# Decode attention values as float32 on four column tiles, with unsplit V and loads in pools of their own

## The chip, the cores and the metric

The kernel runs on one core of one Trainium2 chip. TensorE multiplies matrices, VectorE and ScalarE do elementwise work and reductions, GpSimd does small elementwise work and issues some DMAs, SyncE issues the other DMAs. The metric is the device time of one execution in microseconds, as the median of several runs. The program is recorded by a layer that orders the instructions of each engine at build time, with priorities and a planned timeline; on the chip each engine then runs its own list strictly in that order and waits on semaphores.

## What is computed

One step of a streaming encoder with two layers, for 1024 new frames of one prompt stream and for 16 new frames of each of 8 running streams (the decode part). The change concerns layer 0 of the decode part only: differential attention of 16 queries per stream against 1024 cached and 16 new keys and values, in 4 heads. Each head has two softmax maps, whose difference weighs the values:

```python
def _diff_attn(q, k, v, q_pos, k_pos, rel_bias, lam):
    s = jnp.einsum('bqhcd,bkhcd->bhcqk', q, k).astype(jnp.float32) * (A_HALF_DIM ** -0.5)
    bias = rel_bias[_t5_bucket(k_pos[None, :] - q_pos[:, None])]
    s = s + jnp.transpose(bias, (2, 0, 1)).astype(jnp.float32)[None, :, None]
    ...
    p = jax.nn.softmax(s, axis=-1)
    w = p[:, :, 0] - lam * p[:, :, 1]
    return jnp.einsum('bhqk,bkhe->bqhe', w.astype(v.dtype), v)
...
    o = _rmsnorm(o, subln_g) * (1.0 - LAMBDA_INIT_0)
    out_a = o.reshape(bsz, t, A_WIDTH) * jax.nn.silu(g_a)
    ...
    y = x + jnp.einsum('bte,ed->btd', jnp.concatenate([out_a, out_b], axis=-1), w_out)
```

All inputs are float32. The cached keys and values of one stream are 2 MiB each, and every one of them is read once from HBM.

## The kernel before

The program goes through the input projection, the attention and gating of the prompt (`phase_prompt`), the decode stage (`phase_decode`, prepared by `decode_begin`), and the convolution layer (`phase_conv`). Large products are done in the type float32r, with each operand split into a high and a low part and three products per pair (`mm3`, line 157). Small products are done in float32, and each of these shows as two instructions in the trace.

The decode stage does two things at once. The first is the attention of the eight streams, called sequences here. The second is the output projection of layer 0 for the tiles of 128 tokens: `prep` loads and transposes a tile, `main` multiplies it (48 products of 512 columns, tile "out"), adds the residual and normalises. One pass of the loop over b, a period, takes scores of sequence b, keys of b+1, values of b-1, the projection of tile b-2 and the weights of b. The steps of a sequence are:

- `keys_part`: four loads of 512 KiB from the key cache into tiles "raw", issued by SyncE. These tiles come from the pool `rawp` of three buffers, which the loads of the output weights (`split_w`, line 139) and of `prep` share. TensorE transposes them (line 417), and VectorE and ScalarE copy the result to KT.
- `dscores`: scores of the 4 heads, each head on its own 32 columns of TensorE, so on four column tiles (line 731), in three PSUM tiles S; then maxima (736), exponents (744) and sums.
- `dweights`: nine products of the exponents with `cf`, which holds the normaliser and the sign of each map, give the weights with the keys on the partitions (759), 64 columns for 4 heads of 16 queries. They are split into a high and a low part (762, 763).
- `dvalues`: four loads of V into "vraw", two buffers, issued by GpSimd (773). ScalarE makes the high part vh (776), VectorE the low part vl (777). The weights of all heads are multiplied with all 512 columns of V (784, 785, 787), so that three quarters of the result belong to a wrong head; a mask `own` takes them out (789), a product with `place` moves the sequence to its rows (791), and VectorE adds it to `oacc` (795).
- `dfinish`: once for all sequences, the norm per head, the gate from `s_ga`, and the store to `s_oa`, which `prep(8)` reads.

The product of weights and values in the code is this:

```python
                    if k < 8:
                        nc.tensor.matmul(pav, lhsT=wt[:, k, :], rhs=x, start=(k == 0), stop=False)
                    nc.tensor.matmul(pav[:64], lhsT=wt[:, k, :64], rhs=y, start=False, stop=False)
```

What sets the order around it is the recording order of the loop, moved by the planned timeline: the trace of before shows the value products of one sequence in several pieces between "out" products and key transposes, and the scores of a sequence in up to five pieces.

## Time and profile before

| | us |
|---|---|
| median of 3 runs (lowest, highest) | 1223.09 (1223.04, 1224.46) |
| profiled execution | 1223.68 |
| its span, first to last instruction | 1221.9 |
| TensorE busy in the span | 1156.0 |
| VectorE, ScalarE, GpSimd busy | 731.6, 456.8, 340.7 |
| mean granted clock of TensorE, as a share of 2.4 GHz | 0.979 |

The times of the runs are of whole executions; the profile is of one more execution, and its span leaves out 1.8 us before the first and after the last instruction. A matmul's record lasts longer than its share of TensorE, since matmuls are pipelined, so costs are read from the distance of starts. "Idle" in a row is the time in which an engine did nothing just before an instruction, with what released it.

### The profile page before, as it was taken

What the parts mean: (1) busy time and instruction counts of PE and PEld (TensorE: products, weight loads), DVE (VectorE), ACT (ScalarE), POOL (GpSimd) and SP (SyncE); (2) the same over time, 40 slices, a digit from 0 to 9 for tenths busy, and PEclk for the clock granted to TensorE, in tenths of its full rate; (3) what the DMA queues carried; (4) which work ended last, traced back from release to release, by engine and by line L of the source; (5) the groups of instructions that cost most, each with busy time, mean ns of one, the idle gap of its engine ahead of it and who ended that gap; (6) DMA issues with size and microseconds to landing.
All of it is one profiled execution on the core that took longest, in us unless ns stands there. A gap on an engine that the chain in (4) does not pass through costs nothing. (4 is left out here: it accounts for less than half of the span.)

```text
span 1221.9 us, 20908 instructions
## 1 busy us (share of the span) xinstructions
PE 1156.0 (95%) x7886; PEld 1024.1 (84%) x7886; DVE 731.6 (60%) x1560; ACT 456.8 (37%) x1065; POOL 340.7 (28%) x510
## 2 busy tenths in 40 slices
PE   6999999999989998679999999999999999998997
PEld 4878998899989997457777677899999899996886
DVE  4420225678788878766556444698999711377443
ACT  4431223445454545555444334312121222365221
POOL 2233223334434435413322231212131220350000
PEclk9999999999989998879999999999999999998999
DMA  8453435324132313867767635333332442113331
GB/s 302 110 169 91 144 118 172 107 71 121 46 89 78 108 50 105 301 214 242 258 226 255 192 125 190 92 91 96 93 96 90 140 134 84 35 35 104 104 104 69
DMA packets 125365, 160.33 MB, mean 131 GB/s; under 512 B 16514, under 2 KB 87194, under 8 KB 125257
## 3 DMA queue, kind: packets, MB, share of 16 engines
q1 hardware_dynamic: 109344, 106.95, 28.5%
q0 software_dynamic: 15776, 51.79, 12.9%
q8 instruction: 62, 1.02, 0.3%
q14 instruction: 39, 0.31, 0.1%
q10 hardware_dynamic: 144, 0.26, 0.1%
HBM read 119.41 MB, written 40.00 MB: 130 GB/s over the span
## 5 line engine op out<-in xcount | busy, mean ns | idle before, releaser
L157 PE MATMUL mm<-yh,wh 128*128 128x384 f32 x576 | 196.5, 341 | 3.3 <-ACT sb L1133 2.5
L157 PE MATMUL mm<-yl,wh 128*128 128x384 f32 x576 | 193.9, 337 | 0.5 <-issue 0.5
L157 PE MATMUL mm<-yh,wl 128*128 128x384 f32 x576 | 193.8, 338 | 0.3 <-DVE wl L146 0.2
L157 PE MATMUL mm<-wh,xh 128*128 128x384 f32 (+1 forms) x504 | 185.4, 369 | 2.5 <-DVE sg L468 1.4
L157 PE MATMUL mm<-wl,xh 128*128 128x384 f32 (+1 forms) x504 | 184.5, 366 | 0.9 <-DVE wl L146 0.9
L157 PE MATMUL mm<-wh,xl 128*128 128x384 f32 (+1 forms) x504 | 183.7, 364 | 0.0
L146 DVE TENSOR_TENSOR wl<-raw,wh 128x1024 fp32r<-128x1024 f32 (+1 forms) x72 | 84.3, 1178 | 104.7 <-ACT wh L145 102.7
L1173 DVE SCALAR_TENSOR_TENSOR cT<-u,cc,cT 128x128 f32<-128x128 f32 (+1 forms) x180 | 141.3, 843 | 1.0
L157 PEld LDWEIGHTS mm<-yh,wh 128*128 128x128 f32 x576 | 108.7, 189 | 6.2 <-issue 2.8
L157 PEld LDWEIGHTS mm<-yh,wl 128*128 128x128 f32 x576 | 108.6, 189 | 2.0 <-DVE wl L146 0.9
L157 PEld LDWEIGHTS mm<-yl,wh 128*128 128x128 f32 x576 | 108.7, 189 | 1.1 <-issue 0.7
L157 PEld LDWEIGHTS mm<-wh,xh 128*128 128x128 f32 x504 | 95.7, 190 | 13.3 <-DVE sg L468 1.4
L157 PEld LDWEIGHTS mm<-wl,xh 128*128 128x128 f32 x504 | 95.9, 190 | 10.5 <-DVE wl L146 1.8
L157 PEld LDWEIGHTS mm<-wh,xl 128*128 128x128 f32 x504 | 95.7, 190 | 8.7 <-DVE xl L170 0.3
L145 ACT CAST wh<-raw 128x1024 fp32r<-128x1024 f32 (+1 forms) x72 | 71.8, 1001 | 73.0 <-PE mm L157 30.9
L126 POOL TENSOR_TENSOR rr<-pw,mhalf 128x1 f32<-128x1 f32 x59 | 33.0, 559 | 200.3 <-DVE pw L125 190.8
L559 ACT ACTIVATE e<-S,nm 128x512 f32<-128x512 f32 (+5 forms) x96 | 55.1, 579 | 42.1 <-DVE nm L554 26.4
L157 PE MATMUL out<-wh,ch 128*128 128x512 f32 x144 | 59.9, 416 | 2.0 <-DVE xr L845 1.2
L157 PE MATMUL mm<-wh,ch 128*128 128x512 f32 x144 | 57.1, 397 | 4.5 <-ACT ch L1079 4.5
L551 DVE TENSOR_REDUCE nm<-S 128x1 f32<-128x512 f32 (+5 forms) x96 | 52.5, 551 | 12.6 <-PE S L546 11.9
L777 DVE TENSOR_TENSOR vl<-vraw,vh 128x1024 fp32r<-128x1024 f32 x32 | 43.2, 1351 | 26.8 <-ACT vh L776 26.6
L157 PE MATMUL out<-wh,cl 128*128 128x512 f32 x144 | 58.8, 408 | 0.0
(282 smaller groups left out, 2300.6 us busy)
## 6 DMA issues: line engine op xcount, KB each, us to landing
raw<-in_cache_k SPq DMA_DIRECT2D x32, 512.0 KB, 4.4
vraw<-in_cache_v POOLq DMA_DIRECT2D x32, 512.0 KB, 5.7
raw<-in_w_in SPq DMA_DIRECT2D x24, 512.0 KB, 5.3
raw<-in_w_out SPq DMA_DIRECT2D x16, 512.0 KB, 5.0
raw<-in_w_in SPq DMA_DIRECT2D x32, 256.0 KB, 4.0
raw<-in_w_in SPq DMA_DIRECT2D x48, 128.0 KB, 2.8
s_y<-xr POOLq DMA_DIRECT2D x9, 512.0 KB, 4.7
x<-s_y SPq DMA_DIRECT2D x9, 512.0 KB, 4.3
```

The source lines that it names most:

```text
L126: m = nc.gpsimd.tensor_tensor(out, v[:, :w], self.mhalf[:, :w], ALU.pow)
L145: nc.scalar.copy(h[:, :ks * n], raw[:, :ks * n])
L146: (low or nc.vector).tensor_tensor(l[:, :ks * n], raw[:, :ks * n], h[:, :ks * n].bitcast(F32), ALU.subtract)
L157: m = self.nc.tensor.matmul(out, lhsT=x, rhs=y, start=(i == 0), stop=(i == n - 1))
L551: nc.vector.tensor_reduce(nm[:, j:j + 1], s[:, :n], AX.X, ALU.max, negate=True)
L559: nc.scalar.activation(e[:, j * n:(j + 1) * n], S[j][:, :n], AF.Exp, bias=nv, accum_out=zz[:, j:j + 1])
L777: (nc.vector if i in VDVE else nc.gpsimd).tensor_tensor(vl, vr, vh.bitcast(F32), ALU.subtract)
L1173: nc.vector.scalar_tensor_tensor(dst, src, w1, dst, ALU.mult, ALU.add)
```

## The change

The value product no longer works with split operands. V is used as it is loaded, the weights are kept as one float32 tile, and each head's 16 weight columns are multiplied with its own 128 columns of V only, on the column tile of that head, so that no mask and no placing are needed: the result of a sequence stands with head h at partitions 32h to 32h+15. The norm and the gate are done for each sequence right behind its values, from a gate tile `gs` in the same layout, and `og` is stored to `s_oa` in two portions. The sum over keys runs backwards (the new keys' tile first, then tiles 7 to 0).

The four score products are called in one group with a higher priority, the values too. Key loads get a pool of five buffers of their own (`krp`), value loads one of six (`vp`), now allocated on the other side of the memory, and `vload(b)` is called behind `dvalues(b - 1)`, `vload(0)` ahead of the loop. The pool of PSUM tiles for the weights falls from two buffers to one; one PSUM tile `pvt` holds two value results and two ninth weight columns. The constants `own` and `place` are no longer loaded.

```diff
+HPS = 300
+VB = 6
+KB = 5
...
-        vp = E(tc.tile_pool(name="vp", bufs=2, side="right", reuse_waits="tile"))
+        krp = E(tc.tile_pool(name="krp", bufs=KB, side="right", reuse_waits="tile"))
...
+            nc.gpsimd.memset(gs, 0.0)
+            for h in range(H):
+                nc.sync.dma_start(out=gs[h * 32:h * 32 + NQ], in_=self.s_ga[T:, h * P:(h + 1) * P].rearrange(
+                    "(b q) e -> q b e", q=NQ))
+            nc.sync.dma_start(out=vs, in_=self.v0s)
...
-                kr = self.rawp.tile([P, 1024], F32, name="raw").rearrange("p (t c) -> p t c", t=2)
+                kr = krp.tile([P, 1024], F32, name="kraw").rearrange("p (t c) -> p t c", t=2)
...
+        vp = dec.enter_context(tc.tile_pool(name="vp", bufs=VB, reuse_waits="tile"))
+        pm = E(tc.tile_pool(name="pa", bufs=1, space=PSUM, reuse_waits="tile"))
+        pvp = E(tc.tile_pool(name="pvp", bufs=1, space=PSUM, reuse_waits="tile"))
+        pvt = pvp.tile([P, 512], F32, name="pv")
...
-            for i, parts in enumerate(((0, 1), (2,), (3,))):
-                s = pS.tile([P, 512], F32, name="S")
-                for j, p in enumerate(parts):
+            S = [pS.tile([P, 512], F32, name="S") for _ in range(3)]
+            with tc.high_priority(offset=HPS):
+                for p, i, j in ((3, 2, 0), (2, 1, 0), (0, 0, 0), (1, 0, 1)):
...
-            wt = ep.tile([P, 9, P], F32R, name="wt", bufs=1)
...
+            wt = ep.tile([P, 9, 64], F32, name="wt", bufs=2)
+            ps = pm.tile([P, 512], F32, name="mm")
+            p8 = pvt[:, 256 + b % 2 * 64:320 + b % 2 * 64]
+            for k in range(9):
+                nc.tensor.matmul(ps[:, k * 64:(k + 1) * 64] if k < 8 else p8, lhsT=ex[:, k, :], rhs=cf,
+                                 start=True, stop=True)
+            nc.scalar.copy(wt[:, :8], ps.rearrange("p (k e) -> p k e", e=64))
+            nc.vector.tensor_copy(wt[:, 8], p8)
...
+        def vload(b):
...
+            for i in range(4):
+                vr = vp.tile([P, 1024], F32, name="vraw").rearrange("p (t c) -> p t c", t=2)
+                nc.gpsimd.dma_start(out=vr, in_=cv[:, 2 * i:2 * i + 2])
+                seqs[b]["V"] += [vr[:, 0], vr[:, 1]]
...
+            pav = pvt[:, b % 2 * P:(b % 2 + 1) * P]
+            with tc.high_priority(offset=HPS):
+                for k in range(8, -1, -1):
+                    for h in range(H):
+                        nc.tensor.matmul(pav[h * 32:h * 32 + NQ], lhsT=wt[:, k, h * NQ:(h + 1) * NQ],
+                                         rhs=V[k][:, h * P:(h + 1) * P], start=(k == 8), stop=(k == 0))
             jk = ep.tile([P, P], F32, name="jk", bufs=1)
...
+            nc.scalar.activation(jk, pav, AF.Square, accum_out=ss)
...
             self.rpow(rm, ss, 1.0 / P, 1e-6)
...
+            nc.vector.scalar_tensor_tensor(og[:, b], pav, rm, gs[:, b], ALU.mult, ALU.mult)
+            if b >= NB - 2:
...
+                    nc.sync.dma_start(out=self.s_oa[T:, h * P:(h + 1) * P].rearrange("(b q) e -> q b e", q=NQ)[:, bs],
+                                      in_=og[h * 32:h * 32 + NQ, bs])
...
+        vload(0)
         for b in range(NB):
...
                 dvalues(b - 1)
+                vload(b)
...
-        dfinish()
```

Where the instructions come to stand is told by the built programs. TensorE at the opening of the decode stage, before: S is a score tile, `tr<-cst,raw` key transposes, and the rows on lines 784 and 785 are the values of sequence 0.

```order
L417 MATMUL tr<-cst_58,raw 128x128 x8
L731 MATMUL S<-KT,qz_5782 32x256 x4
L784 MATMUL mm<-vh,wt 128x512
L785 MATMUL mm<-vl,wt 64x512
L784 MATMUL mm<-vh,wt 128x512
L785 MATMUL mm<-vl,wt 64x512
L784 MATMUL mm<-vh,wt 128x512
L417 MATMUL tr<-cst_58,raw 128x128 x8
L731 MATMUL S<-KT,qz_5782 32x256 x4
L785 MATMUL mm<-vl,wt 64x512
```

The same place now: lines 739, 766 and 789 are scores, weights and values.

```order
L766 MATMUL mm<-cf,ex 128x64 x8
L766 MATMUL pv<-cf,ex 128x64
L739 MATMUL S<-KTx,qz_5782 32x272 x4
L789 MATMUL pv<-vs,wt 16x128 x4
L789 MATMUL pv<-vraw,wt 16x128 x32
L739 MATMUL S<-KT,qz_5782 32x256 x12
L766 MATMUL mm<-cf,ex 128x64 x8
L766 MATMUL pv<-cf,ex 128x64
L789 MATMUL pv<-vs,wt 16x128 x4
L789 MATMUL pv<-vraw,wt 16x128 x32
L766 MATMUL mm<-cf,ex 128x64 x2
L170 MATMUL tr<-cst_58,raw 128x128 x4
```

The values of a sequence now stand in one piece, the scores in one group but for the piece of the last keys here, and the values of sequences 0 and 1 both stand ahead of the first "out" product. GpSimd behind the exponents' zeroing of sequence 1, before, with the semaphores that each row waits for:

```order
L739 MEMSET ex_6178 128x128 [waits PE_49,Activation_49,Pool_49]
L773 DMA vraw_6432<-in_cache_v0 128x2x512 [waits DMASW7_49,DVE_49]
L773 DMA vraw_6442<-in_cache_v0 128x2x512 [waits DMASW0_49,DVE_49]
L704 COPY KTx_6559<-kts_5774 128x4x16
L773 DMA vraw_6452<-in_cache_v0 128x2x512 [waits DMASW7_49,DMASW1_49,DVE_49]
```

The same place now:

```order
L746 MEMSET ex_6194 128x128 [waits PE_49,Activation_49]
L779 DMA vraw_6298<-in_cache_v0 128x2x512 [waits DMASW1_49,PE_49]
L779 DMA vraw_6300<-in_cache_v0 128x2x512 [waits DMASW2_49,PE_49]
L779 DMA vraw_6492<-in_cache_v0 128x2x512 [waits DMASW3_49,PE_49]
L779 DMA vraw_6494<-in_cache_v0 128x2x512 [waits DMASW4_49,PE_49]
```

A value load waited for VectorE's split of the buffer's last contents; now it waits for TensorE's last product with them. vraw_6298 and vraw_6300 are the last two of sequence 1 and reuse buffers of sequence 0.

## Rows read from the trace of the kernel before

**Rows 1.** The page: busy us of each engine, share of the span, instructions.

```profile
PE 1156.0 (95%) x7886; PEld 1024.1 (84%) x7886; DVE 731.6 (60%) x1560; ACT 456.8 (37%) x1065; POOL 340.7 (28%) x510
```

**Rows 2.** Stretches: busy PE, PEld, DVE, ACT, POOL (instructions), clock, DMA share, GB/s.

```profile
508.00:550.00 42.00, 28.25 (x198) 17.86 (x196) 26.31 (x44) 21.47 (x41) 7.86 (x16) 0.80 0.75 252
550.00:690.00 140.00, 139.18 (x834) 102.58 (x833) 81.27 (x137) 64.32 (x126) 42.88 (x59) 1.00 0.73 239
```

**Rows 3.** Order in time: start, us, engine, line, operation, count; opening, late wait.

```profile
511.12 0.64 PE L731 MATMUL S<-KTx,qz 128*32 128x272 f32 x8
...
518.59 0.31 DVE L750 TENSOR_SCALAR cf<-mk,z,sgn 128x64 f32<-128x64 f32 x1
...
520.27 2.73 PE L759 MATMUL mm<-cf,ex 128*128 128x64 f32 x18
...
549.66 0.50 PE L157 MATMUL out<-wh,ch 128*128 128x512 f32 x1 [0.24 <-ACT ch L169]
...
696.24 0.63 PE L157 MATMUL out<-wl,ch 128*128 128x512 f32 x1
696.67 0.63 PE L157 MATMUL out<-wh,cl 128*128 128x512 f32 x1
```

**Rows 4.** Order in time, TensorE: scores, values, placing products, weights.

```profile
508.36 1.07 PE L731 MATMUL S<-KT,qz 128*32 128x256 f32 x16
...
561.27 0.40 PE L787 MATMUL mm<-vs,wt 128*128 128x512 f32 x1
561.60 0.64 PE L731 MATMUL S<-KT,qz 128*32 128x256 f32 x8
562.17 1.09 PE L417 MATMUL tr<-cst,raw 128*128 128x128 f32 x8
...
565.94 1.02 PE L791 MATMUL mm<-om,mk 128*128 128x512 f32 x2
...
575.66 0.40 PE L785 MATMUL mm<-vl,wt 128*64 128x512 f32 x1
...
577.05 0.39 PE L785 MATMUL mm<-vl,wt 128*64 128x512 f32 x1
...
612.28 1.02 PE L791 MATMUL mm<-om,mk 128*128 128x512 f32 x2
613.14 1.22 PE L759 MATMUL mm<-cf,ex 128*128 128x64 f32 x10
...
689.71 1.02 PE L791 MATMUL mm<-om,mk 128*128 128x512 f32 x2
```

**Rows 5.** All weight loads of scores: ns min/median/max, first and last start.

```profile
L731 PEld LDWEIGHTS S<-KT,qz x192: 106/109/178, 508.4 to 679.4; 128*32 128x32 f32 x192
```

**Rows 6.** Order in time: weight loads and matmuls of one score group.

```profile
573.18 0.16 PEld L731 LDWEIGHTS S<-KT,qz 128*32 128x32 f32 x8
573.18 0.64 PE L731 MATMUL S<-KT,qz 128*32 128x256 f32 x8
```

**Rows 7.** What TensorE waited for from 480 to 775: total us, times, longest.

```profile
PE mm L784 <- DVE wt L763: 5.4, 1, 5.4
PE S L731 <- ACT ex L744: 4.9, 1, 4.9
...
PE tr L417 <- DMA raw<-in_cache_k: 2.0, 1, 2.0
...
PE mm L759 <- DVE oacc L795: 1.6, 1, 1.6
...
PE S L731 <- DVE gah L596: 1.2, 1, 1.2
```

**Rows 8.** DMA issues from 490 to 720: count, KB each, median us to landing.

```profile
vraw<-in_cache_v POOLq DMA_DIRECT2D x29, 512.0 KB, 5.8
...
raw<-in_w_out SPq DMA_DIRECT2D x8, 512.0 KB, 6.7
```

**Rows 9.** The busiest ten microseconds of the DMA engines, columns as in rows 2.

```profile
510.00:520.00 10.00, 4.45 (x48) 1.78 (x48) 7.40 (x15) 5.05 (x11) 2.29 (x5) 0.73 1.01 369
```

More of the change, by code (lines that the diff above doesn't have):

```diff
@@ L754, in dweights @@
             ex, cf = seqs[b]["ex"], seqs[b]["cf"]
-            wt = ep.tile([P, 9, P], F32R, name="wt", bufs=1)
-            for g0, g1 in ((0, 8), (8, 9)):
-                ps = pm.tile([P, 512], F32, name="mm")
-                for k in range(g0, g1):
-                    nc.tensor.matmul(ps[:, (k - g0) * 64:(k - g0 + 1) * 64], lhsT=ex[:, k, :], rhs=cf,
-                                     start=True, stop=True)
-                pv = ps[:, :(g1 - g0) * 64].rearrange("p (k e) -> p k e", e=64)
-                nc.scalar.copy(wt[:, g0:g1, :64], pv)
-                nc.vector.tensor_tensor(wt[:, g0:g1, 64:], pv, wt[:, g0:g1, :64].bitcast(F32), ALU.subtract)
@@ L797, in dfinish @@
-        def dfinish():
-            ss = self.small.tile([P, H], F32, name="ss4")
+            wt = ep.tile([P, 9, 64], F32, name="wt", bufs=2)
[5 more added lines that the diff above has]
+            nc.scalar.copy(wt[:, :8], ps.rearrange("p (k e) -> p k e", e=64))
@@ L802, in dfinish @@
-            rm = self.small.tile([P, H], F32, name="rm")
+            ss = self.small.tile([P, 1], F32, name="ss")
+            nc.scalar.activation(jk, pav, AF.Square, accum_out=ss)
+            rm = self.small.tile([P, 1], F32, name="rr")
             self.rpow(rm, ss, 1.0 / P, 1e-6)
-            ga = vp.tile([P, 1024], F32, name="vraw", bufs=2)[:, :512]
-            nc.sync.dma_start(out=ga, in_=self.s_ga[T:, :])
-            for h in range(H):
-                hs = slice(h * P, (h + 1) * P)
-                nc.vector.scalar_tensor_tensor(ga[:, hs], oacc[:, hs], rm[:, h:h + 1], ga[:, hs],
-                                               ALU.mult, ALU.mult)
```

63 lines of the change are left out of this document (17 added, 46 removed).

## Prediction

> **What bounds the kernel now.** I read the page's busy times first, then busy time by stretch, then the instruction groups and the order in time inside the stretch that the change touches, then who waited for whom, then the DMA. TensorE is busy 95% of the span [rows 1]. By stretch, the decode stage (from the first decode scores at 508.36 to the convolution's first products near 770) has two kinds of time. From 550 to 690 TensorE is busy 139.18 of 140 us at the full clock, while VectorE is busy 81.27 and the DMA engines 0.73 of the time [rows 2]: there an instruction less on TensorE is time less, and work taken off VectorE or ScalarE is worth nothing by itself. Before that, from 508 to 550, TensorE is busy 28.25 of 42 us at a mean granted clock of 0.80 [rows 2]: the opening is bound by a chain of softmax, weight and load steps, and with its idle gaps part of it runs at 1.2 instead of 2.4 GHz. The first product of the output projection ("out") starts at 549.66 [rows 3], and I split the sum there. The order is unchanged up to the last gate products of the prompt near 480, and the stage after it is paced by TensorE again, so it moves up with the end of this one.
>
> **Term 1: the product of weights and values, on the path.** Before, a sequence costs 18 float32r matmuls of 512 columns (lines 784, 785, 787) that start 0.232 us apart (six starts from 575.66 to 577.05), and one float32 product that places the result (line 791), two instructions and 0.86 us from its start to the next line's [rows 4]. That is 18 x 0.232 + 0.86 = 5.04 us. Seven of the eight sequences have it after 549.66: 7 x 5.04 = 35.2 us.
>
> After, it is 36 float32 matmuls of 128 columns, in nine groups of four heads on four column tiles, two passes each as with every float32 product here. No row shows this form. The nearest is the score product (line 731), of the same type and on the same four column tiles, with 256 columns. Sixteen of its instructions take 1.07 us and eight take 0.64 [rows 4], so eight more, two passes of four tiles, cost 0.43 us, or 0.215 per pass: the four tiles run side by side, at two cycles of the full clock per column. With 128 columns that is 0.107 us per pass, if weights arrive in time. A score load lasts 0.106 to 0.110 us [rows 5], about as long as the new pass, so a pass may have to wait for its load. Eight score loads start within 0.05 us of each other (done in 0.16 [rows 6], each lasting 0.11), four within some 0.03, so 0.107 + 0.03 = 0.137 is the upper end when load and pass overlap. I take the middle, 0.125: 9 x 2 x 0.125 = 2.25 us. Going into column tiles and out again costs time too: 0.33 instead of 0.23 us on the way in (561.27 to 561.60), and eight score instructions last 0.57 to the next line (561.60 to 562.17) instead of 0.43 [rows 4]. That is about 0.24 us a visit. A sequence's values so cost x = 2.5 us, between 2.2 and 2.7 if loads are hidden. Six sequences have it after the first "out" (the order puts two ahead): 6x = 15.
>
> One rule speaks against this. The Trainium skill, "TensorE: Matmul & The Clock Gate", section "Part 3: Packing small matmuls — row/col tiling", The mechanism, says that a weight load overlaps matmuls in flight only when it targets other row groups; these tiles differ in columns alone. The rows do not bear it out for scores: eight loads are done within 0.16 us of a group that lasts 0.64, so the second four lie under the first four's matmuls [rows 6]. By the rule a pass would be load plus matmul; that result is rival 2.
>
> **Term 2: visits to column tiles.** For sequences 3 to 7 the scores were scattered: 23 visits after 549.66, of which the first is at 561.60 [rows 4]. In one group they are 5. 18 x 0.24 = 4.3 us gained. The visits of the values are in x.
>
> **Term 3: the wait at 693.6.** TensorE waited 1.6 us for VectorE to add the placed output, since the weights needed its PSUM buffer [rows 7]; behind it the clock was low and some eight products started 0.43 us apart (696.24, 696.67) [rows 3], 8 x 0.2 = 1.6. Neither the placement nor the addition is left, and the next user of the weights' buffer waits only for a ScalarE copy of one period ago: 3.1 us gained.
>
> **Term 4: the opening.** Its waits were 5.4 us for the split of the weights, 4.9 for exponents, 2.0 for a key load and 1.2 for the last prompt output [rows 7], 13.5 us in sum. A mean clock of 0.80 between two levels means 40% of the time at the lower; if that falls on busy and idle time alike, 11.3 of the 28.25 busy us [rows 2] ran at half speed, and 5.6 are lost. At best all of it goes, about 19 us; at worst the opening stays as long. Which waits are next? Softmax of sequence 0 stays: from the end of the scores at 511.76 (511.12 and 0.64) to the normaliser that ends at 518.90 it took 7.1 us [rows 3], with output-weight splits of VectorE in it, which stay. Then come the weights, 2.7 at the low clock (520.27 [rows 3]), their copy, about 0.9, and the values, 3.3 at a mixed clock; then the last two V loads of sequence 1 may start, since they reuse the buffers of sequence 0's, and take 5.8 to land [rows 8] after some 0.4 for issue; then its values 2.5 and the rest of sequence 2's weights, about 1.5: 511.8 + 24.2 = 536. A chain of equal length runs over the output weights: three rounds of load (6.7 to landing [rows 8]) and split, and ScalarE has those casts ahead of its copy of the second weights. I take 537.5, so 12 us gained, with both sequences' values already in it.
>
> **Hidden or small.** Splitting V into two parts (cast on ScalarE, difference on VectorE) is 32 pairs that go; between 550 and 690 they lay under TensorE. The new per-sequence normalisation (square, power on GpSimd, scale) stands after the values and nobody waits for it for most of a period, except that the ninth weight column writes the same PSUM tile: in the opening it waits for sequence 0's, about 2 us inside the chain above. GpSimd's queue now holds six V loads ahead of two small steps of the prompt's gate, and SyncE four more loads ahead of the keys: 1 to 2 us in a prompt tail that waits on other things; I put nothing. If that cover is gone, it costs these 2.
>
> **Term 5: new waits.** A period is 24.8 us (the placing products at 565.94 and 689.71 are five apart [rows 4]); it falls to about 22, while its bytes stay. At 239 GB/s [rows 2] 24.8 us are 5.9 MB; in 22 us that needs 269 GB/s. For 10 us the engines reached 369 at a share of 1.01 [rows 9], but over the 42 us of the opening 252 [rows 2]. I expect late loads now and then: 4 us lost, between 0 and 16.
>
> **Sum.** Gain = 12 - 2(x - 2.5) + 35.2 - 6x + 4.3 + 3.1 - 4 = 55.6 - 8x. With x = 2.5 it is 35.6 us. The profiled execution took 1223.7 (its span is 1221.9, with 1.8 around it), the median of the runs is 0.6 less; 1223.7 - 35.6 - 0.6 = 1187.5, say 1188.
>
> **Rivals.** (1) *Loads become the bound.* K and V have their own pools, but pools add no bandwidth. If the stage is held at the 252 GB/s of the opening [rows 2], a period is 5.9/0.252 = 23.4 us, 1.4 more than forecast, and over six periods 8 us are lost, with half of the opening's gain (6) as that chain is loads: 1188 + 14 = 1202, less the 4 already counted, 1198; at the 239 of the middle [rows 2] the periods would gain nothing, and 6 + 3 are left: 1214. For it: the share of 1.01 at 510 [rows 9]. Against: TensorE waited for key or value loads 2.0 us in all [rows 7]. The Trainium skill ("Trainium Kernel Development and Optimization", Key Constraints) says that loads issued from SyncE and GpSimd run on the same 16 engines; no row here shows them apart. (2) *Weight loads are not hidden* in passes half as long: x = 9 x 2 x (0.107 + 0.107) + 0.24 = 4.1, gain 22.8, time 1200. For: load and pass are equally long. Against: the score rows [rows 6]. (3) *Slower: the four tiles run one after another*, by their accumulation into one PSUM tile or their 16 columns. Then 72 instructions at about 0.11 us, the spacing of short float32 products (ten within 1.22 at 613.14 [rows 4]), give x = 8.2: gain -10.0, time 1233. It decides from x = 7.0 on (55.6/8), that is 0.75 us per group of four. Against: the score form shows one group in 0.43 with twice the columns. (4) *The opening does not shorten*, since the key transposes of sequence 2 stand ahead of the first scores and wait for 9 key loads and 6 V loads in the same queue: 1200.
>
> **How the numbers follow.** Forecast 0.57 (1188; its own bounds are x 2.2 to 2.7, opening 5 to 19, new waits 0 to 9, not all at one end: 1175 to 1199). Rival 1 0.16, rival 2 0.11, rival 4 0.09, rival 3 0.05; 0.02 for a loss elsewhere that cancels the gain. The range 1174 to 1206 takes in the forecast and most of 1, 2 and 4. Faster 0.93, same 0.02, slower 0.05, where 0.2% (2.4 us) is about what a measurement of this kernel can tell from no change.
>
> **What would show it.** Right: the value matmuls of a sequence (36 x 2 instructions) within 2.2 to 2.7 us, four starting within 0.03 us; one group of scores per sequence; first "out" before 542; TensorE at 99% busy behind it, with periods of 22 us; no wait for VectorE before the last weights. Wrong: tiles that start one by one (rival 3), 0.2 us or more between passes (rival 2), waits of TensorE for kraw or vraw in most periods (rival 1), scores of sequence 0 after 516 (rival 4).

## The result and the profile after

| | before | after |
|---|---|---|
| median (lowest, highest), us | 1223.32 (1223.04, 1224.46) | 1209.28 (1205.85, 1212.23) |
| profiled execution | 1223.68 | 1205.85 |
| its span | 1221.9 | 1204.1 |

The changed kernel takes 0.988 of the time before (95% interval 0.9858 to 0.9902), 14 us less; forecast were 1188 us, 35 less, in a range of 1174 to 1206. The sign was right, the size was not. The profiled execution is the quickest of four, 3.4 us under their median, and gains 17.8 us; the prediction's sum is compared with it, since that sum was made against the profiled execution of before.

The page of the kernel after, as in [rows 1]:

```profile
PE 1131.1 (94%) x8302; PEld 1015.9 (84%) x8302; DVE 681.8 (57%) x1515; ACT 423.4 (35%) x1032; POOL 339.2 (28%) x517
```

TensorE is 24.9 us less busy, VectorE 49.8 and ScalarE 33.4. Where the work went is plain; where the time went is told by three landmarks of the timeline, the first and the last "out" product and the end of TensorE:

| | before | after | gain | forecast |
|---|---|---|---|---|
| start to the first "out" | 549.66 | 551.79 | -2.1 | 12 |
| first to last "out" | 202.36 | 176.19 | 26.2 | 23.6 |
| last "out" to the end of TensorE | 462.42 | 469.03 | -6.6 | 0 |

The sum of the gains is 17.5. So the part that the change works on gained 2.6 us more than forecast, the opening gave 14 us less, and a stage that the change doesn't touch, the convolution, lost 6.6.

**The values.** TensorE of the kernel after in order of time (start, us, engine, line, operation, count), one sequence in the middle; weight loads (PEld) and matmuls (PE), `vs` being the new values and `vraw` the cached ones:

```profile
588.20 0.41 PE L789 MATMUL pv<-vs,wt 128*16 128x128 f32 x8
588.32 1.75 PEld L789 LDWEIGHTS pv<-vraw,wt 128*16 128x16 f32 x64
588.42 1.93 PE L789 MATMUL pv<-vraw,wt 128*16 128x128 f32 x64
590.28 0.50 PE L160 MATMUL out<-wl,ch 128*128 128x512 f32 x1
```

From 588.20 to 590.28 a sequence takes 2.08 us; the mean of the sequences at full clock is 2.09. That is 18 passes of 0.109 us and 0.12 that is left for the visit. All the loads of that time fit under the passes, and each lasts about as long as the pass of four tiles that it stands under (ns min/median/max):

```profile
L789 PEld LDWEIGHTS pv<-vraw,wt x512: 97/97/151, 536.2 to 681.0; 128*16 128x16 f32 x171
```

**The stretches**, columns as in [rows 2]:

```profile
500.00:530.00 30.00, 23.48 (x187) 17.46 (x187) 18.94 (x49) 13.64 (x34) 8.72 (x22) 0.87 1.00 350
508.00:550.00 42.00, 32.00 (x370) 23.92 (x369) 25.92 (x58) 22.47 (x55) 12.70 (x26) 0.88 0.94 332
550.00:690.00 140.00, 133.66 (x1231) 108.55 (x1229) 47.68 (x112) 46.01 (x110) 45.13 (x65) 1.00 0.67 234
```

From 508 to 550 TensorE is busier than before and its clock higher, but the DMA engines went from a share of 0.75 and 252 GB/s [rows 2] to 0.94 and 332. From 500 to 530 they are full; before, they stood there at a share of 0.74 and 246 GB/s.

From 550 to 690 TensorE is now idle for 6.3 us instead of 0.8 [rows 2]. Its waits from 560 to 690 (tile and line that waited, releaser; total us, times, longest; KT and KTx are the copies of the transposed keys, KTx the one that the new keys are added to, and rr is a step of GpSimd's power):

```profile
PE S L739 <- POOL rr L129: 2.7, 4, 0.7
PE tr L420 <- ACT KT L421: 1.4, 5, 0.4
PE S L739 <- ACT KTx L421: 0.9, 1, 0.9
PE out L160 <- ACT ch L172: 0.9, 1, 0.9
PE tr L420 <- DVE KT L421: 0.5, 1, 0.5
```

None is for kraw or vraw, the loads of keys and values.

**The opening**, TensorE of the kernel after, to be set beside [rows 3]:

```profile
500.96 1.97 PE L420 MATMUL tr<-cst,kraw 128*128 128x128 f32 x8 [5.36 <-DMA kraw<-in_cache_k]
...
518.61 0.67 PE L739 MATMUL S<-KTx,qz 128*32 128x272 f32 x8
519.85 1.50 PE L739 MATMUL S<-KT,qz 128*32 128x256 f32 x24 [0.57 <-DVE gah L599]
...
535.13 1.11 PE L739 MATMUL S<-KTx,qz 128*32 128x272 f32 x8 [2.81 <-ACT ex L751]
535.95 0.72 PE L789 MATMUL pv<-vs,wt 128*16 128x128 f32 x8
...
545.92 3.35 PE L789 MATMUL pv<-vraw,wt 128*16 128x128 f32 x64 [1.63 <-DMA vraw<-in_cache_v]
...
551.79 0.48 PE L160 MATMUL out<-wh,ch 128*128 128x512 f32 x1
```

The scores of sequence 0 end at 521.3 instead of 511.8, so the opening is 9.5 us late from the outset. Two things end close together there: the key transposes, which wait 5.36 us for the first key load at 500.96 and are through at 518.6, and the last gate products of the prompt (gah is their gate tile), for which the scores at 519.85 still wait, since they need their PSUM. SyncE's issues tell why. First the kernel before, then after (SPq is the queue of SyncE):

```profile
419.78 0.38 SPq L697 DMA_DIRECT2D raw<-in_cache_k  x1
...
429.76 0.54 SPq L697 DMA_DIRECT2D raw<-in_cache_k  x1
...
487.44 0.41 SPq L697 DMA_DIRECT2D raw<-in_cache_k  x1
...
500.44 0.38 SPq L577 DMA_DIRECT2D gah<-s_ga  x1
...
505.83 0.34 SPq L577 DMA_DIRECT2D gah<-s_ga  x1
```

```profile
495.25 3.17 SPq L702 DMA_DIRECT2D kraw<-in_cache_k  x5
...
502.96 9.59 SPq L702 DMA_DIRECT2D kraw<-in_cache_k  x5
513.23 0.38 SPq L580 DMA_DIRECT2D gah<-s_ga  x1
514.65 0.46 SPq L580 DMA_DIRECT2D gah<-s_ga  x1
```

Before, the first two key loads left at 420 and 430, since the shared pool `rawp` is open all the time; in the kernel after, loads of the output weights stand in those places. The own pool gets its memory from tiles of the input projection: in the built program its first load waits for TensorE's last product there (mm), which ends at 480.79:

```profile
480.45 0.34 PE L160 MATMUL mm<-wh,xl 128*128 128x384 f32 x1
```

The load leaves only at 495.25, because it stands in SyncE's queue behind the small loads of the decode stage, four of which are new, those of the gate tile gs. The queue's own waits for them, from 480 to 520:

```profile
SPq L679 <- DMA gs<-s_ga: 2.2, 1, 2.2
...
SPq L680 <- DMA gs<-s_ga: 2.0, 1, 2.0
SPq L678 <- DMA gs<-s_ga: 1.5, 1, 1.5
```

That is 5.7 us of the 14.5 from 480.8 to 495.25. The last two gate loads of the prompt (gah) stand behind key loads in the same queue and leave 13 and 9 us later than before. And six V loads have been put on the same DMA engines ahead of the keys by GpSimd:

```profile
482.61 2.94 POOL L779 DMA_DIRECT2D vraw<-in_cache_v  x4
...
485.83 1.44 POOL L779 DMA_DIRECT2D vraw<-in_cache_v  x2
```

From 480 to the first "out" the kernel before moves 17.8 MB, the kernel after 22.9. Loads issued from 480 to 552 (count, KB each, median us to landing):

```profile
kraw<-in_cache_k SPq DMA_DIRECT2D x17, 512.0 KB, 7.2
...
vraw<-in_cache_v POOLq DMA_DIRECT2D x14, 512.0 KB, 8.3
...
raw<-in_w_out SPq DMA_DIRECT2D x6, 512.0 KB, 8.4
```

Before, the same loads took 4.6, 5.2 and 6.7 us from 480 to 552.

### The profile page after: what moved, and what is told of

Same layout as the page of the kernel before. It is cut to its first block, busy times and chain, and to the rows that moved or that the text cites. A ratio compares the mean times of both kernels' runs of the same rounds, so it can differ in the third digit from the quotient of the medians.

```text
span 1204.1 us, 21623 instructions
## 1 busy us (share of the span) xinstructions
PE 1131.1 (94%) x8302; PEld 1015.9 (84%) x8302; DVE 681.8 (57%) x1515; ACT 423.4 (35%) x1032; POOL 339.2 (28%) x517
## 5 line engine op out<-in xcount | busy, mean ns | idle before, releaser
L129 POOL TENSOR_TENSOR rr<-pw,mhalf 128x1 f32<-128x1 f32 x67 | 37.1, 555 | 204.3 <-DVE pw L128 195.9
L160 PE MATMUL mm<-wl,ch 128*128 128x512 f32 x144 | 57.4, 398 | 0.7 <-DVE wl L149 0.7
```

Of the source, the lines that this page charges most:

```text
L129: m = nc.gpsimd.tensor_tensor(out, v[:, :w], self.mhalf[:, :w], ALU.pow)
L160: m = self.nc.tensor.matmul(out, lhsT=x, rhs=y, start=(i == 0), stop=(i == n - 1))
```

## Experiments

A letter stands for a theory in the expectations. Of the 6.6 us of the convolution: A, they come from a new order of VectorE there; B, from single late transfers. Of the opening: C, the sum of the bytes sets it; D, its chain of steps does; E, the order of its loads; F, the gate load behind the key loads; G, the bytes ahead of the first eight key loads; J, the own key pool that opens late. Of the period's new waits: H, they are for ScalarE's copy of KTx behind the square of the norm; I, for GpSimd's power. Each ratio is to the kernel before on the same chip, with its 95% interval; medians of one table may come from different chips. Line numbers differ by a few between these kernels. Landmarks are of one execution each, and two kernels that were run twice differ in them by up to 4 us.

### The convolution: 6 us from one place in VectorE's order

In the last part of the convolution VectorE takes back tile 6 from a store and load (cT<-big) and makes tile 7's last third (big, utmp), on which the last filter products wait. The planner put the first ahead of the second in the kernel after, and behind it in the kernel before. The edit, **conv**, undoes this alone; **after2** is the changed kernel a second time, **conv2** is conv a second time beside it:

```diff
                 if i == 0:
-                    back(6)
+                    with tc.issue_after(self.last_u):
+                        back(6)
...
-                nc.vector.tensor_tensor(utmp, pa_[:, 224:384], sb[:, 224:], ALU.mult)
+                mu = nc.vector.tensor_tensor(utmp, pa_[:, 224:384], sb[:, 224:], ALU.mult)
+                self.last_u = mu.ins if hasattr(mu, "ins") else mu
```

> The changed kernel with one VectorE order restored in the convolution: taking back the filtered tile 6 stands behind the last third of tile 7 and its tap buffer, as before, and not ahead of them. Theory A (the planner's new order there costs what was lost behind the decode stage): utmp of tile 7 ends some 5 us earlier against the TensorE products around it, the wait of 3.3 us of the last filter group for big<-s_u falls under 1 us, from the last out product to the end it is 462 to 464 us instead of 469.0, and the time is about 1203 us (1209.3 for the changed kernel). Rival B (the 6.6 us are late DMA round trips that would come in any order): that stretch stays at 467 to 470 and the time at 1207 to 1211.

> The changed kernel itself, on the same chip as the next. Theory A: 0.988 of before, and from the first transpose of the convolution to the end some 445 us.

> conv again, on the same chip as the changed kernel. Theory A: 5 to 7 us below the changed kernel, and from the first transpose of the convolution to the end 438 to 441 us. Rival B: within 2 us of the changed kernel.

conv took 1202.21 us (0.9812, 0.9784 to 0.9839). On one chip after2 took 1206.56 (0.9853, 0.9828 to 0.9877) and conv2 1200.39 (0.9800, 0.9776 to 0.9824): 6.2 us less, the intervals apart, with the opening and the periods equal (first "out" at 550.14 and 550.27, last at 726.30 and 726.54). VectorE in order of time, after2 and then conv2:

```profile
973.65 1.21 DVE L1209 TENSOR_SCALAR cT<-big,cc 128x1024 f32<-128x1024 f32 x1 [4.51 <-DMA big<-s_c]
...
975.64 0.33 DVE L1139 TENSOR_TENSOR utmp<-mm,sb 128x160 f32<-128x160 f32 x1
```

```profile
970.20 0.34 DVE L1140 TENSOR_TENSOR utmp<-mm,sb 128x160 f32<-128x160 f32 x1
...
973.88 1.22 DVE L1211 TENSOR_SCALAR cT<-big,cc 128x1024 f32<-128x1024 f32 x1 [3.33 <-DMA big<-s_c]
```

In after2 tile 7's last third stands behind an instruction that waits 4.51 us for a transfer. In conv2 it goes ahead, utmp is there 5.4 us earlier, and TensorE's waits for the loads of this kind in the whole convolution fall from 8.1 us to 3.6 (after2, then conv2):

```profile
PE py L1190 <- DMA big<-s_u: 8.1, 3, 4.7
```

```profile
PE py L1192 <- DMA big<-s_u: 3.6, 2, 2.3
```

A holds for most of the loss. The stretch from the last "out" to the end of TensorE is 471.5 us in after2, 465.2 in conv2 and 465.8 in conv, not the 462 to 464 that was expected, and 462.4 in the kernel before. What is left, some 3 us, was not traced; open3_hps0 below has the order of conv there on every engine and takes 468.7, so it is no more than executions of one order differ by. Nothing in the diff touches this stage; the planned timeline in front of it changed, and the planner chose again. All kernels below have this edit too, so they are compared with conv and conv2.

### The periods: the priority, not the loads

**c_hps0** takes the priority of scores and values away, **ktx_dve** has VectorE copy all of KTx, **c_kb3** gives the key pool three buffers instead of five, **kshare** leaves out the own pool and puts the key loads back into the shared pool of three:

```diff
-HPS = 300
+HPS = 0
...
-                    (nc.scalar.copy if j else nc.vector.tensor_copy)(...)
+                    (nc.scalar.copy if j and i < 3 else nc.vector.tensor_copy)(...)
...
-KB = 5
+KB = 3
...
-                kr = krp.tile([P, 1024], F32, name="kraw").rearrange("p (t c) -> p t c", t=2)
+                kr = self.rawp.tile([P, 1024], F32, name="raw").rearrange("p (t c) -> p t c", t=2)
```

> As conv, and without the priority of scores and values, so that the planner may scatter them again. If grouping is worth what was forecast (0.24 us a visit of the column tiles): with some 15 to 25 more visits a period of 23.0 us grows by 0.6 to 1 us and the time is 4 to 6 us above conv. If the priority itself holds up the opening or the new waits of 0.9 us a period (TensorE for rr, KTx, KT ahead of the group): those waits vanish, the periods stay or shrink, and the time is 0 to 6 us below conv.

> As conv (the order on TensorE is the same), but both halves of the last key tile are copied by VectorE, not one of them by ScalarE. Theory H (the new wait of 0.67 us ahead of each score group is for ScalarE's copy, which stands behind the square of the output norm, 1.25 us, and the new square of the values, 0.46 us): the waits of TensorE before the score groups fall from 0.67 to 0.2 to 0.4 us, a period from 23.0 to 22.6 to 22.7, and the time is 2 to 3 us below conv. Rival I (it waits for GpSimd's power step, as the row names it): the waits and the time stay within 1 us of conv.

> As conv, with three own key buffers instead of five. Theory C: fewer keys asked for ahead of the first out product (some 22 MB instead of 24), which comes at 548 to 550. Periods: the keys need four loads each and three buffers refill as TensorE transposes, so if five were more than needed, the periods stay at 23.0 and the time is 2 to 4 us below conv; if three hold the transposes up as the shared pool did (3.1 us a period), periods of 25 to 26 and a time 10 us or more above conv.

> As conv, with one part of the change undone: the keys are loaded into the shared pool of three buffers again, not into five of their own. Theory C and F: fewer key loads are asked for ahead, so gah comes earlier and fewer bytes stand ahead of the first out product (20 to 21 MB instead of 24): scores of sequence 0 at 511 to 515, first out at 545 to 549. The periods: if own key buffers are worth something there, a period grows from 23.0 by the waits for keys (2.0 us in all in the kernel before), and the time is within 3 us of conv; if they are worth nothing, the time is 4 to 7 us below conv.

| | median, us | ratio | four periods, us | first "out" |
|---|---|---|---|---|
| conv2 (own pool of five, priority) | 1200.39 | 0.9800 (0.9776 to 0.9824) | 92.0 | 550.27 |
| c_hps0 | 1197.91 | 0.9777 (0.9744 to 0.9810) | 88.3 | 553.26 |
| ktx_dve | 1202.26 | 0.9811 (0.9781 to 0.9841) | 90.5 | 549.61 |
| c_kb3 | 1203.06 | 0.9815 (0.9792 to 0.9838) | 92.0 | 554.76 |
| kshare | 1224.78 | 0.9993 (0.9970 to 1.0015) | 108.5 | 559.73 |

(Before: 105.4 for four periods. The values of three sequences stand ahead of the first "out" in kshare, of two or little more in the others.) The new waits of 2.7 us are put down to GpSimd in the list above. But in conv, ScalarE's last instructions ahead of such a group are these, and TensorE starts 0.15 us after the copy has ended:

```profile
594.89 1.06 ACT L178 ACTIVATE yn<-xr 128x1024 f32<-128x1024 f32 x1
...
595.94 0.27 ACT L793 ACTIVATE jk<-pv 128x128 f32<-128x128 f32 x1
...
596.19 0.58 ACT L421 COPY KTx<-tr 128x512 f32<-128x512 f32 x1
```

```profile
596.92 0.67 PE L739 MATMUL S<-KTx,qz 128*32 128x272 f32 x8 [0.67 <-POOL rr L129]
```

GpSimd's step ends at 596.88, close to this too, so these rows don't part H from I. ktx_dve does, where VectorE makes the copy:

```profile
614.19 0.67 PE L739 MATMUL S<-KTx,qz 128*32 128x272 f32 x8 [0.33 <-DVE pw L128]
...
614.19 1.08 POOL L129 TENSOR_TENSOR rr<-pw,mhalf 128x1 f32<-128x1 f32 x2 [0.77 <-DVE pw L128]
```

The scores start while GpSimd's step only starts, so they don't wait for it: I is out. The waits in front of score groups halve, from 0.67 to 0.33 us each, and a period falls from 23.0 to 22.63: H holds for that half; the rest is a wait for VectorE, whose copy of KTx ends at 614.05. In c_hps0 the 3.6 us of waits in four periods are gone, with periods of 22.07. These are its waits for score groups in the same stretch:

```profile
PE S L739 <- ACT KTx L421: 0.2, 1, 0.2
```

Its values stand in three visits and take 2.42 instead of 2.09 us a sequence, its scores stay in one group. So the priority saves less in visits than it costs in waits, and four periods are 3.7 us shorter without it. In time that is 2.5 us against conv2, from another chip, and 4.3 against conv on the same chip, and the intervals meet: the trace shows the mechanism, the medians alone don't settle it. Its periods move 263 GB/s at a DMA share of 0.75, more than the 234 and 0.67 of the kernel after from 550 to 690.

kshare shows what the own pool is for. The first key loads leave at 419 again and the scores start at 511.82, but in the periods TensorE waits for the keys, whose loads wait for buffers:

```profile
PE tr L420 <- DMA raw<-in_cache_k: 9.3, 3, 3.8
```

With other waits TensorE is idle for 14.7 us in four periods, and the whole gain is lost. Three own buffers are as good as five in the periods.

### The opening: its late start, and what follows when it is mended

Edits, in the order of the expectations. **c_vb4**: four V buffers instead of six. **c_vlate**: the first V loads issued behind GpSimd's copy of qz. **halfv**: half of each V row loaded for the first three sequences and used twice, so it leaves out half of their values and serves only to take bytes away. **open2**: V, gs and vs loaded behind the copy of KTx of sequence 1, and gs and vs by GpSimd instead of SyncE. **gah_first**: key loads from sequence 2 on only behind the last gate load. **open3**: open2 and gah_first. **k01**: the first two key loads from the shared pool.

```diff
-VB = 6
+VB = 4
...
+            with tc.issue_after(self.qz0): vload(0)
...
+                w = 256 if b < 3 else 512
+                nc.gpsimd.dma_start(out=vr[:, :, :w], in_=cv[:, 2 * i:2 * i + 2, :w])
...
+            with tc.issue_after(seqs[1]["kx"]): vload(0); self.setup2()
...
+                if b > 1: es.enter_context(tc.issue_after(self.gah_m))
...
-                kr = krp.tile(
+                kr = (self.rawp if b == 0 and i < 2 else krp).tile(
```

> As conv, and with four value buffers instead of six, so that only the four value loads of sequence 0 stand ahead of the first keys, and later ones are asked for a sequence later. Theory C (the opening is bound by how many bytes are asked for ahead of what is needed): scores of sequence 0 some 3 to 4 us earlier than 518.6, first out product at about 546 instead of 551.8, time 5 to 6 us below conv. Rival D (the opening is bound by the chain of softmax, weights and values of sequences 0 and 1, both ahead of the first out product): first out within 1 us of 551.8, time as conv, or above it if value loads come late in the periods.

> As conv, and the six value loads stand behind the copy of the first queries on GpSimd, so behind the loads of biases, queries and the first keys. Theory E (the order of the loads delays the start): the first key load lands at 493 to 495 instead of 500.9, scores of sequence 0 start at 508 to 511, the first out product at 541 to 545, time 8 to 10 us below conv. Theory C, in its strong form (the amount of bytes ahead of the first out product, some 22 MB at 340 GB/s, and not their order): scores of sequence 0 come earlier, but the first out product stays at 549 to 552 and the time within 2 us of conv. Rival D: the whole chain moves with the scores, as E.

> As conv, but of the values of sequences 0, 1 and 2 only the first 256 of 512 columns are loaded (the products use these columns twice; this leaves out half of the data of three sequences). That takes 3.1 MB from the loads up to 560 us; the number of loads and of products stays. The planner, seeing shorter loads, puts the first out product ahead of the values of sequence 1. Theory C strong (the sum of bytes asked for ahead of the first out product, at 320 to 350 GB/s, decides): first out at 543 to 546 instead of 552.8, the last out product 6 to 8 us earlier than conv's 730.2, time 6 to 8 us below conv. Rival D (the chain of softmax, weights and values): only the move of the values past the first out product shows, last out at 728 to 731 and the time within 2 us of conv.

> As conv, with the six first value loads, the loads of the gates and of the new values all behind the copy of the last keys of sequence 1 on GpSimd: nothing that the scores do not need stands ahead of the eight key loads of sequences 0 and 1. Theory G (the opening starts late because of 3 MiB of values and five small loads ahead of the eight key loads): the first key load is issued at 489 to 491 instead of 495.6, the scores of sequence 0 start at 508 to 511 instead of 518.2, and as the values land while the softmax runs, the first out product comes at 541 to 545 instead of 552.8; time 8 to 10 us below conv. Theory C strong (what counts is the sum of bytes ahead of the first out product, 23 to 24 MB at 320 to 350 GB/s, in whatever order): scores of sequence 0 earlier, first out still at 548 to 552, time within 3 us of conv.

> As conv, with one order on SyncE changed: the key loads of sequence 2 and later stand behind the last gate load of the prompt (gah), of which three stood ahead of it. Theory F (the first scores start late because their PSUM banks come free only after the last gate load, which stands in SyncE's queue behind key loads that wait for buffers and for the saturated DMA engines): no wait of TensorE for gah, the key transposes of sequence 2 no longer ahead, scores of sequence 0 at 515 to 517 instead of 518.2 (the eight keys ahead of them land by then), first out 550 to 552, time 0 to 3 us below conv. Theory C strong: time within 1 us of conv.

> As open2 (values, gates and new values behind the eight key loads), and with the order of gah_first. In open2 the first scores waited 6.4 us for gah and 4.4 us for a key of sequence 2, both of which stand behind them now. Theories F and G together: scores of sequence 0 at 509 to 513 (518.1 in conv), first out at 543 to 547, time 6 to 9 us below conv, 0.975 of before. Theory C strong (the sum of bytes ahead of the first out product decides): scores of sequence 0 at 509 to 513, but first out at 549 to 553 and the time within 3 us of conv.

> As conv, but the first two key loads of sequence 0 go into the shared pool again, all others into the five own buffers. Theory J (the own key pool opens late: its memory is free only when the prompt's last gate products are done, so that the first two key loads and their transposes, at 420 and 430 us before, stand behind the small loads at 495 us now, in the stretch whose DMA engines are full): these loads are issued at 419 and 429 again, the eight keys that the first scores wait for land 3 us earlier, scores of sequence 0 at 514 to 516 instead of 518.2 to 519.4, first out 547 to 550, time 2 to 4 us below conv. Rival F alone (the last gate load, which still stands behind nine key loads, holds the first scores): TensorE waits for gah instead, scores at 517 to 519, time within 1 us of conv.

| | median, us | ratio | MB to the first "out" | first "out" | last "out" | TensorE's longest wait |
|---|---|---|---|---|---|---|
| before | | | 17.8 | 549.7 | 752.0 | |
| conv | 1202.21 | 0.9812 | 24.2 | 552.8 | 730.2 | key load 4.8 |
| conv2 | 1200.39 | 0.9800 | 22.8 | 550.3 | 726.5 | key load 4.8 |
| c_vb4 | 1204.49 | 0.9832 | 20.5 | 546.9* | 727.0 | key load 4.9 |
| c_vlate | 1213.19 | 0.9905 | 23.3 | 560.1 | 738.0 | load of s_oa 6.0, gah 5.4 |
| halfv | 1196.25 | 0.9758 | 19.1 | 546.9* | 726.1 | gah 5.8 |
| open2 | 1206.59 | 0.9849 | 23.5 | 558.7 | 734.5 | gah 6.4 |
| gah_first | 1204.70 | 0.9831 | 22.4 | 553.1 | 728.5 | cf 6.3 |
| open3 | 1208.99 | 0.9851 | 22.2 | 550.4 | 728.2 | key load 7.8 |
| k01 | 1199.42 | 0.9792 | 20.4 | 542.8* | 721.0 | gah 5.0, key load 5.0 |

(* The values of sequence 1 stand behind the first "out" there, some 3 us of work that the others have ahead of it. The intervals are about 0.003 to each side, 0.9732 to 0.9783 for halfv, 0.9751 to 0.9833 for k01 and 0.9790 to 0.9912 for open3.)

In k01 the two loads leave at the old times and the first score products start at 514.41 instead of 518.6:

```profile
419.10 0.37 SPq L702 DMA_DIRECT2D raw<-in_cache_k  x1
```

That shows that the late key loads make the first group of scores late (J). But the gain is then eaten by the next wait, for the gate load behind the key loads, and the scores of sequence 0 end at 523.4, no earlier than in the kernel after:

```profile
PE tr L420 <- DMA kraw<-in_cache_k: 7.1, 3, 5.0
...
PE S L739 <- DVE gah L599: 5.0, 1, 5.0
```

The one kernel whose scores end early is kshare (514.8): with three buffers fewer key loads stand ahead of the gate loads too, which leave at 503.8 and 507.2. Its first "out" is no earlier for it, at 559.7. Where the gate load is put first (gah_first), the scores end at 519.0, the wait for gah is gone, and another takes its place, for the normaliser of sequence 0 on VectorE:

```profile
PE mm L770 <- DVE cf L761: 6.3, 1, 6.3
```

And where V, gs and vs go out of the way (open2), the first key load leaves 5 us earlier, at 490.29, and TensorE waits more for keys than in conv (4.8 us) all the same:

```profile
PE tr L421 <- DMA kraw<-in_cache_k: 9.9, 3, 4.4
...
PE S L744 <- DVE gah L600: 6.4, 1, 6.4
```

What E and G forecast did not come: c_vlate should have had its first "out" at 541 to 545 and has it at 560.1, with its last gate load behind nine more key loads, so that it leaves at 522.5; open2 (541 to 545) has it at 558.7, and open3, with F's order besides (543 to 547), at 550.4.

So J and F are true of single waits, and none of them alone sets the end. C stands as a bound that is never far: over the whole opening these kernels move 286 to 333 GB/s, and the shares are 0.81 to 0.95. But C is not the whole either: halfv moves 3.7 MB less than conv2, 11 us at its rate, and its last "out" is 0.4 us earlier. What halfv gains in the median, 4 us against conv2 on the same chip, lies behind the last "out" in the traces (461.4 us there against 465.2), where executions of one order took 465.2 to 468.7. What sets the first "out" at 546 to 560 whatever stands first in the queues (k01's 542.8 is 546 with the values of sequence 1) stays open; D is not shown either, since no order of the loads that was tried took the chain of steps clear of waits.

### Combinations

**hps0_vb4**, **open2_hps0_vb4**, **open3_hps0** and **k01_gf_hps0** put the edits of their names together (gf is gah_first), in search of a kernel that beats both:

> As conv, without the priority and with four value buffers. The two edits act at different places (periods and opening). If what four buffers gave the opening (first out 5.9 us earlier) was lost again because the values of sequence 1 moved behind the first out product (2.1 us) and an idle opening of other kinds, the time is within 2 us of the kernel without the priority alone (0.978 of before). If the two add up, it is 4 to 6 us below that.

> open2, without the priority and with four value buffers. Theory G: scores of sequence 0 at 508 to 511, first out at 538 to 543, periods of 22.1 us, time 1185 to 1190 (0.97 of before). Theory C strong: fewer bytes ahead of the first out product (21 instead of 24 MB) bring it to 545 to 548, and the time is 1192 to 1196 (0.976).

> open3 without the priority of scores and values. Periods of 22.1 us as in the kernel without the priority alone (no wait of TensorE ahead of the score groups), and the opening of open3. Theories F and G: time 1188 to 1192 on a chip where before takes 1223 (0.973). Theory C strong: 1194 to 1198 (0.978), no better than without the priority alone.

> k01 with the gate loads ahead of the key loads of sequence 2 and without the priority of scores and values. Theories F and J: scores of sequence 0 at 512 to 515, no wait for gah, first out 545 to 549; periods of 22.1 us as without the priority; time 0.973 to 0.975 of before (1193 to 1195 where before takes 1226), below every kernel so far. If the sum of bytes ahead of the first out product decides instead: first out at 551 to 554 and 0.977 to 0.978.

| | median, us | ratio | first "out" | last "out" |
|---|---|---|---|---|
| hps0_vb4 | 1199.56 | 0.9786 (0.9755 to 0.9817) | 544.9* | 721.4 |
| open2_hps0_vb4 | 1226.46 | 1.0008 (0.9988 to 1.0029) | 556.9 | 757.2 |
| open3_hps0 | 1206.98 | 0.9848 (0.9806 to 0.9890) | 559.2 | 732.1 |
| k01_gf_hps0 | 1197.70 | 0.9777 (0.9739 to 0.9815) | 554.1 | 726.4 |

(* As in the table of the opening.)

None of them reached what the sum of its edits was expected to give. hps0_vb4 and k01_gf_hps0 came out as expected for the case that the edits don't add up; for k01_gf_hps0 that case was theory C's (551 to 554 and 0.977 to 0.978). In k01_gf_hps0 the wait for the gate is gone, and one of 6.3 us for the weights (wt, VectorE) and one of 6.8 for a key load stand in its place. open3_hps0 gains nothing over open3. open2_hps0_vb4 lost everything, and shows what visits to column tiles cost: its values stand in ten visits a period instead of c_hps0's three, eight of them right behind "out" products, and its periods take 25.65 instead of 22.07 us with hardly a wait (0.3 us in four). That is 0.51 us a visit. Half of it is in the values' own time (4.24 us a sequence instead of 2.42), the rest in the neighbours: an "out" product takes 0.43 us to the start of a value product and 0.23 to that of another "out". The best kernels that compute everything, c_hps0 and k01_gf_hps0, take 1197.9 and 1197.7 us, 0.978 of the time before, where the changed kernel took 0.988 and 0.985.

## Why the prediction was right in sign and wrong in size

**Term 1, right, and better than its middle.** x was 2.09 us, under the lower end of 2.2: the pass is 0.109, as worked out from the score rows [rows 4] without the addition for load starts, and the visit 0.12, besides 0.09 in the "out" product ahead of it (0.32 us to the next start instead of 0.23). After the first "out" the values fell from 34.87 to 12.53 us; forecast were 20.2 of gain, it was 22.3. The four tiles run side by side, which ends rival 3, and the loads are hidden, which ends rival 2: four matmuls start 5 to 8 ns apart, the next four 90 ns later, and a load lasts 97 ns. The rule in the Trainium skill ("TensorE: Matmul & The Clock Gate", "Part 3: Packing small matmuls — row/col tiling") that a load overlaps only matmuls on other row groups is not borne out by these rows either; by it a sequence's values would have taken 4.1 us, by the estimate of rival 2.

**Term 2, right in size.** The scores fell by 4.1 us, forecast 4.3. Scattered, the five sequences took 13.5 us in 22 visits (the prediction counted 23), in one group each 9.5 in five: 0.24 a visit, as forecast.

**Term 3, right.** The wait of 1.6 at 693.6 [rows 7] is gone, and the "out" products, some at the low clock before, are 2.5 us shorter in sum; forecast 3.1 for both, 4.1 found. Two small items that the sum doesn't have make up the rest of the 26.2: the weights took 2.9 us less, 16 of their products now standing ahead of the first "out", and the transposes 1.8 more.

**Term 5, right in size, wrong in cause.** I put 4 us for late loads. From first to last "out" TensorE's idle time rose from 5.5 to 9.3 us although 1.6 had gone, so 5.4 are new; no wait for a key or a value load is among those from 560 to 690. All but 0.9 of these are for copies of the transposed keys, and they came from the priority that the change gives the scores: without it they are gone (c_hps0). That the size fits is luck. I had worked out what the group of scores saves and not what it waits for when it is pulled forward. Rival 1 lost its main ground with that: bandwidth does not hold the periods, which run at a share of 0.67 and can run at 0.75 (c_hps0).

**Term 4, the step that failed.** I took the scores of sequence 0 to end at 511.8 as before, and moved the steps behind them. They end at 521.3, 9.5 us later; from there to the first "out" it is 30.4 us where the prediction has 25.7, with one wait of 2.8 at 535.13 in it. The sentence that "the order is unchanged up to the last gate products of the prompt near 480" was false for SyncE from 419 on, and the step said in passing that "SyncE four more loads ahead of the keys: 1 to 2 us in a prompt tail that waits on other things; I put nothing". Three things were missing in it. The pool that a load's buffer comes from decides when the load may leave: the first two key loads were at 420 and 430 before, which stood in the issue list of SyncE, and the own pool has its memory at 480.8. The queue then holds the load to 495.25, and 5.7 us of that are waits for those four loads (gs), which I put at nothing. And loads were drawn forward into the stretch: 22.9 MB instead of 17.8 up to the first "out", at 319 GB/s 16 us more for the DMA engines, in a stretch that had a quarter of them free. Rival 4 named the effect (scores after 516, 1200 us) with other particulars and a chance of 0.09, which was too low. The experiments show that the late key loads make the first group of scores late (k01: 514.4 instead of 518.6), and that undoing this alone leaves the end of the scores where it was, at the gate load. In k01 it is worth some 5 us of the opening (last "out" 721.0 against 726.5) and nothing certain in the median. They do not show what holds the rest; that cause stays open.

**The stage behind, a step that was taken for granted.** "The stage after it is paced by TensorE again, so it moves up with the end of this one" was false by 6.6 us, most of it one place in VectorE's order: undoing it gives back 6.2 us in the median (conv2 against after2), and 3.3 to 6.3 in this stretch of the traces (465.8 and 465.2 against 469.0 and 471.5). The prediction looked at the decode stage alone.

Of the miss of 17.8 us in the profiled execution 14.1 are term 4's, 6.6 the convolution's, and 2.6 were won back by terms 1, 2, 3 and 5; the rest, 0.3, lies behind TensorE's end. The median adds 3.4, since that execution is the quickest.

## What to carry to other kernels

Giving loads a pool of their own changes when the first of them may leave, and which loads they then stand ahead of: compare the issue times of each queue's first loads before counting what comes behind them, count the small loads that the queue has to get through ahead of them, and add up the bytes that move into the stretch. Where a planner orders the instructions, compare the whole order of each engine, also far from the edit, and ask of each group that a priority pulls forward what it will then wait for. In a stretch with several chains of nearly equal length, one removed wait says little; the next one takes its place.

## What the runs showed of the hardware

- Float32 matmuls on four column tiles with 16 columns of weights and 128 columns of data run at 0.109 us per pass of four, with weight loads of 97 ns hidden under them. That the rows of scores scaled with the columns to within 2% was more than I had expected.
- A visit to column tiles cost 0.24 us for the scores, and 0.51 for the values between "out" products (open2_hps0_vb4 against c_hps0), where the product ahead of it takes 0.43 us to the next start instead of 0.23.
- The DMA engines held 350 GB/s for 30 us (500 to 530), where I had 369 for 10 us at most and 252 over the opening [rows 2, 9]; over the whole opening, at 319 GB/s and a share of 0.93 instead of 251 and 0.76, a 512 KiB load of keys, values or weights landed after 7.2 to 8.4 us instead of 4.6 to 6.7. The Trainium skill ("Trainium Kernel Development and Optimization", Key Constraints) says that loads from SyncE's and GpSimd's queues run on the same 16 engines; the trace agrees, since loads of both queues slow down together (4.6 to 7.2 us on SyncE's, 5.2 to 8.3 on GpSimd's).
